# Two feed-forward chunks woven together, their seven products' shared sums kept in the accumulation banks

## The chip, the cores and the metric

The kernel runs on one core of a Trainium2 chip. The time is the device time of one execution in microseconds (us). The core's engines that matter here are TensorE (PE, the matrix products), VectorE (DVE), ScalarE (ACT), the SyncE queue that issues most transfers (SP) and GpSimd (POOL, which issues the accumulating transfers). Products accumulate in banks of PSUM; everything else lies in SBUF.

## The reference

An encoder trunk of two layers over 512 tokens of width 1024. Each layer mixes tokens in three ways (differential attention, a convolution module, a neighbourhood attention), adds the result to x, then a SwiGLU feed-forward block, then a gated per-layer input. The change touches the feed-forward block, its preparation in the output projection and two flags in the differential attention.

```python
D_MODEL, SEQ, DEPTH = 1024, 512, 2
D_FF = int(math.ceil(8 * D_MODEL / 3 / 256) * 256)          # 2816: 22 chunks of 128
...
        x = x + merged @ w_o[i]
        h = rmsnorm(x, norm_ffn[i])
        x = x + (jax.nn.silu(h @ w_ffn_gate[i]) * (h @ w_ffn_up[i])) @ w_ffn_down[i]
```

All operands are float32.

## The kernel before

Activations lie with the width on the 128 partitions: x and h are eight tiles of 128x512 (tokens along the free side). Every float32 operand of a product is split in a high and a low part (`split`: a copy on ScalarE, a subtraction on VectorE), and a product is three matmuls: high times high, high times low, low times high.

The feed-forward block works on 22 chunks of 128 hidden channels a layer, in three parts of 8, 7 and 7 (`PARTS`). After each part eight down blocks multiply the part's hidden channels with `w_ffn_down` (`gemm`, 128x512 matmuls; the first two as one `pair`), are scaled by the norm (`self.rb`) and added to x.

For one chunk, gate and up (two rows of blocks) times h (two halves of the width by two halves of the tokens) is a 2x2 block product, and `seven` makes it with seven products in place of eight. The weights' sums s1 to s4 and the tokens' sums t1 to t4 (`quarters`, in the output projection) are the operands beside the plain blocks. A product is 4 pairs x 3 = 12 matmuls of 128x256, so a chunk is 84. In the text a product is named by its two operands: "s3 t2" is s3 times t2.

The weights of a chunk come by transfer: s1 and s2 begin as plain loads on SyncE's queue and are completed by accumulating loads on GpSimd's (L987); g (a11, a12) and a22 are plain loads. `halve` splits them: a11/a12 and s1/s2 in rotating buffers `wh` and `wl` (three each, 128x1024), a22 in `kh` and `a`, s3/s4 in two fixed pairs, `pt` for even chunks and `y` for odd ones. s3 and s4 are VectorE sums in a `qk` tile. This preparation has a higher priority by 400 steps (`w_ahead`) than the rest.

The order on TensorE is the order in which the program is written; on the other engines and the transfer queues a scheduler orders the instructions by priority and due time. An engine carries its instructions out in that order.

Before, a chunk's products run without a break in the order a11 b11, a22 t4, s2 t1, a12 b21, s1 t3, s3 t2, s4 b22 (a layer's head chunk in another order). ScalarE copies three of them from their banks to SBUF (p1, p4, p5), and VectorE makes the gate and up sums with seven 128x256 operations (nine in the head chunk). `rest` (Silu, product of gate and up, split) is put off to the next chunk's third product. Chunks take their three banks in turn from the tags `mm, mm, mm` and `sc, sc, av`; `tr` is the tag of the transposition banks, which also serve the norm.

Of the kernel before, what the change touches and what calls it, by code (L numbers as in the profile page):

```python
# [12 lines left out]
F32R = mybir.dt.float32r  # L13
I32 = mybir.dt.int32
AF = mybir.ActivationFunctionType
# [5 lines left out]
P = 128  # L21
# [40 lines left out]
class Net:  # L62
# [109 lines left out]
            self.low = self.split(hi[:, :n], lo[:, :n], raw[:, :n])  # L172
        return hi, lo

    def mm3(self, out, wh, wl, ah, al, first, last):
        mm = self.nc.tensor.matmul
        mm(out, wh, ah, start=first, stop=False)  # L177
        mm(out, wh, al, start=False, stop=False)  # L178
        mm(out, wl, ah, start=False, stop=last)  # L179

    def gemm(self, out, ap, acts, first=True, last=True):

# [88 lines left out]
    def halves(self, h):  # L271
        return h if isinstance(h, tuple) else (h[:, 0, :], h[:, 1, :])

    def norm_chunk(self, k, x, g, tag, st):

        if k == KD - 1:
            self.sumsq(k, x, st)
        h = self.operand(x, g, tag)
        if k < KD - 1:
            self.sumsq(k, x, st)  # L280
        return h
# [562 lines left out]
    def diff_unit(self, head, qt, st4, k2, st, box, ys):  # L844

        nc, i = self.nc, self.i
        half, t = qt // 2, qt % 2
        box[qt] = self.probs(st4, k2, qt, box["s0"])
        if t == 0:
            return  # L850
        yield 3
        ats = [box[2 * half], box[2 * half + 1]]
        pps = []
        for kp in range(2):
            pt = self.ps("tr", (P, 2, 256))
# [12 lines left out]
        cs = slice((head % 2) * P, (head % 2) * P + P)  # L868
        for kp in range(2):
            for u in range(2):  # L870
                v = st["v", head // 2][kp][:, u].rearrange("p (a b) -> p a b", a=2)
                self.mm3(av[:, half * 256:half * 256 + 256], v[:, 0, cs], v[:, 1, cs],
                         pps[kp][:, 0, u], pps[kp][:, 1, u], kp * 2 + u == 0, kp * 2 + u == 3)
# [39 lines left out]
    def w_o(self, mg, xsrc):  # L913
        self.phase = "wo"
        xs, h, st, self.four = [], [], [], []
        self.zs = [self.parts_of("z", [2, 256], 2, F32R) for _ in range(4)]
        for m in range(KD):
            if m % 2 == 0:
                two = self.parts_of("x", [512], 2)
            xo = two[m % 2]  # L920
            self.nc.sync.dma_start(xo, xsrc[m])
            if m == 0:
                both = [self.ps("mm") for _ in range(2)]
                self.pair(both, self.a["w_o"][self.i, 0:2], mg)
# [12 lines left out]
        self.four.append(self.quarters(xs, h, 3))  # L937
        self.main_norm(st[0])
        return xs, h

    def quarters(self, x, h, j):
# [16 lines left out]
        self.tt(t4, t2, b21, ALU.subtract)  # L958
# [10 lines left out]
        return dict(b11=cut(ha, one), b21=cut(hb, one), b22=cut(hb, two),  # L969
                    **{f"t{n + 1}": (o[:, 0], o[:, 1]) for n, o in enumerate(d)})  # L970

    def seven(self, wg, wu, bs, tags, spare, md, first, fb):


        nc = self.nc
        with self.tc.high_priority(offset=min(self.w_ahead, self.tc.cur_priority - self.p0)):
# [34 lines left out]
        def product(out, w, b, first):  # L1011
            wh, wl = ws[w]
            mm = nc.tensor.matmul
            for k in range(4):
                c = slice(k * P, k * P + P)
                bh, bl = bs[k][b]
                mm(out, wh[:, c], bh, start=first and k == 0, stop=False, skip_group_check=True)  # L1017
                mm(out, wh[:, c], bl, start=False, stop=False, skip_group_check=True)  # L1018
                mm(out, wl[:, c], bh, start=False, stop=k == 3, skip_group_check=True)  # L1019
            self.chunk2()  # L1020

        o = self.sb("t", [P, 2, 256])
        p1, p4 = o[:, 0], o[:, 1]
        p5 = self.sb("a", [P, 256])
        gg, uu = self.sb("t", [P, 2, 256]), self.sb("t", [P, 2, 256])
        head = fb == 0
# [12 lines left out]
        product(Q[:, 0], "s1", "t3", False)  # L1039
        product(A[:, 1], "s3", "t2", True)  # L1040
        if head:
            self.tt(gg[:, 0], Q[:, 1], p1, ALU.add)
            self.tt(gg[:, 1], C[:, 0], p5, ALU.add)
        else:
            product(C[:, 0], "s4", "b22", False)
        rb = self.rb.rearrange("p (a b) -> p a b", a=2)
        self.tt(p5, p4, p5, ALU.subtract)
        self.tt(gg[:, 0], gg[:, 0] if head else A[:, 0], rb[:, 0], ALU.mult)
        self.tt(p1, A[:, 1], p1, ALU.subtract)
        self.tt(uu[:, 0], p1, Q[:, 0], ALU.subtract)  # L1050
        self.tt(uu[:, 1], uu[:, 0], p5, ALU.add)
        self.tt(gg[:, 1], gg[:, 1] if head else C[:, 0], p1, ALU.subtract)
        self.tt(gg[:, 1], gg[:, 1], rb[:, 1], ALU.mult)

        def rest(then):
            i = self.act(gg, gg, AF.Silu, table="silu")
# [3 lines left out]
            self.held = self.split(*self.halves(md), gg.rearrange("p a b -> p (a b)"))  # L1060

        self.pending.append(rest)

    def behind(self, i, then):

# [17 lines left out]
    def ffn(self, h, x):  # L1083
# [6 lines left out]
        md8.append(tuple(self.sb("e", [P, 512], F32R) for _ in range(2)))  # L1090
        self.sums, self.sevens = [t for _ in range(2) for t in self.parts_of("qk", [1024], 2)], 0
        for part in PARTS:
            mids = []
            for f, fb in enumerate(part):
                tags = (("mm", "mm", "mm"), ("sc", "sc", "av"))[fb % 2]
                md = md8[f]
                mids.append(md)
                wg, wu = self.a["w_fg"][i, fb], self.a["w_fu"][i, fb]
                self.seven(wg, wu, bs, tags, spare[fb % 2], md, part[0] and f < 2, fb)
            self.flush()  # L1100
            down = [self.a["w_fd"][i, m][:, part[0] * P:(part[-1] + 1) * P] for m in range(KD)]
            two = [self.ps(("mm", "sc")[fb % 2 == 0]) for _ in range(2)]
# [364 lines left out]
```

## Time and profile before

| | |
|---|---|
| median of 3 runs | 1776.36 us |
| range of the runs | 1776.2 to 1777.24 us |
| span of the profiled execution | 1776.7 us |
| TensorE clock granted | 0.999 |
| busy PE, DVE, ACT, POOL | 1767.5, 1421.7, 894.4, 103.0 us |
| feed-forward products, layer 1 | from 495.93 us; down blocks of part 0 from 577.09 us |

No time of the profiled execution but its span is shown; the span lies within the range of the runs. In rows of a timeline the columns are: start, duration, engine, line, operation, what is written and read, and in brackets the idle time before and what ended it. Rows of groups give the busy time, the mean of one in ns, and the idle time before with what ended it. Rows of waits give who waited on whom, the sum in us, how often, and the longest.

### The profile page before, as it was taken

Reading aid. Unit: us, or ns where it says so; the run is one execution under the profiler, and the core shown is the slowest. Engines: PE = TensorE matmul, PEld = TensorE weight load, DVE = VectorE, ACT = ScalarE, POOL = GpSimd, SP = SyncE. Lnnn points to the kernel's source line nnn. Section 1 sums busy time; section 2 is a strip of 40 time slices with the busy share of each in tenths; the row PEclk is TensorE's granted clock in tenths of the full one; section 3 lists DMA queues with packets and bytes.
Section 4 is the critical chain, followed back from the end, with each engine's and each line's share of the span. In section 5 each row is a group of like instructions: output and inputs, shape, how many; then the busy total and the mean of one; then the engine's idle time right before and its main releaser. Section 6 shows DMA issues by size and latency. Waiting matters only on the chain.

```text
span 1776.7 us, 27451 instructions
## 1 busy us (share of the span) xinstructions
PE 1767.5 (99%) x10210; PEld 1559.6 (88%) x10210; DVE 1421.7 (80%) x2418; ACT 894.4 (50%) x1561; POOL 103.0 (6%) x146
## 2 busy tenths in 40 slices
PE   9999999999999999999999999999999999999998
PEld 7888888888899899998888888888888998989987
DVE  7878887998798587787776788889887976867776
ACT  5577555225565254454545765452356643534454
POOL 0000000000111010100000000000001110101000
PEclk9999999999999999999999999999999999999999
DMA  5666641334757366543447655423357664655332
GB/s 202 188 186 176 161 125 42 113 98 140 230 150 193 109 167 160 132 131 123 145 124 198 176 165 149 113 71 95 93 179 198 171 179 115 173 144 151 98 108 92
DMA packets 113509, 256.07 MB, mean 144 GB/s; under 512 B 14560, under 2 KB 19424, under 8 KB 113376
## 3 DMA queue, kind: packets, MB, share of 16 engines
q1 hardware_dynamic: 99984, 229.93, 42.3%
q0 software_dynamic: 12672, 23.07, 8.3%
q8 instruction: 81, 1.33, 0.3%
q10 hardware_dynamic: 720, 1.31, 0.2%
q14 instruction: 52, 0.43, 0.1%
HBM read 215.46 MB, written 7.34 MB: 125 GB/s over the span
## 4 chain that ended last, share of the span: by engine, by line
PE 96%; DVE 2%; ACT 1%; issue 0%; DMA 0%; POOL 0%; ACTq 0%; POOLq 0%; DVEq 0%
PE ffn_mm L1017 4%; PE ffn_mm L1019 4%; PE ffn_mm L177 4%; PE ffn_mm L179 4%; PE ffn_mm L178 4%; PE ffn_mm L1018 4%; PE ffn_sc L1019 3%; PE ffn_sc L1017 3%; PE ffn_sc L1018 3%; PE mergea_mm L177 2%; PE mergea_mm L178 2%; PE mergea_mm L179 2%; PE diff_sc L811 2%; PE gatec_mm L177 2%; PE gatec_mm L178 2%; PE gatec_mm L179 2%
## 5 line engine op out<-in xcount | busy, mean ns | idle before, releaser
L160 DVE SCALAR_TENSOR_TENSOR conv_z<-glu_z,pre_par,conv_z 128x512 f32<-128x512 f32 x240 | 179.4, 748 | 3.3
L143 ACT ACTIVATE ffn_wh<-ffn_wr 128x1024 fp32r<-128x1024 f32 (+1 forms) x92 | 92.7, 1014 | 111.7 <-PE ffn_mm L178 77.1
L987 POOL DMA_DIRECT2D ffn_qk<-w_fu x88 | 78.0, 990 | 605.7 <-DMA ffn_qk<-w_fu 414.7
L157 DVE TENSOR_TENSOR ffn_wl<-ffn_wr,ffn_wh 128x1024 fp32r<-128x1024 f32 (+1 forms) x92 | 107.4, 1173 | 5.4 <-ACT ffn_wh L143 4.9
L157 DVE TENSOR_TENSOR ffn_t<-ffn_mm,wo_rb 128x512 f32<-128x512 f32 (+1 forms) x64 | 38.6, 604 | 67.9 <-PE ffn_mm L179 67.8
L143 ACT ACTIVATE mergea_wh<-mergea_wr 128x1024 fp32r<-128x1024 f32 (+1 forms) x32 | 27.1, 846 | 96.8 <-PE mergea_mm L178 79.6
L143 ACT ACTIVATE ffn_wh<-ffn_qk 128x1024 fp32r<-128x1024 f32 x44 | 46.7, 1060 | 35.9 <-PE ffn_mm L178 15.7
L157 DVE TENSOR_TENSOR ffn_wl<-ffn_qk,ffn_wh 128x1024 fp32r<-128x1024 f32 x44 | 53.8, 1224 | 11.3 <-ACT ffn_wh L143 11.3
L157 DVE TENSOR_TENSOR ffn_t<-ffn_t,ffn_t 128x512 f32<-128x512 f32 (+1 forms) x46 | 31.3, 680 | 31.4 <-ACT ffn_t L143 30.9
L143 ACT ACTIVATE diff_a<-diff_sc,diff_s 128x512 f32<-128x512 f32 x32 | 22.0, 686 | 61.0 <-DVE diff_s L902 61.0
L177 PE MATMUL ffn_mm<-ffn_v,ffn_wh 128*128 128x512 f32 x132 | 51.4, 389 | 0.0
L178 PE MATMUL ffn_mm<-ffn_v,ffn_wh 128*128 128x512 f32 x132 | 51.4, 389 | 0.0
L179 PE MATMUL ffn_mm<-ffn_v,ffn_wl 128*128 128x512 f32 x132 | 51.3, 389 | 0.0
L177 PE MATMUL ffn_mm<-ffn_y,ffn_wh 128*128 128x512 f32 x132 | 51.3, 389 | 0.0
L178 PE MATMUL ffn_mm<-ffn_y,ffn_wh 128*128 128x512 f32 x132 | 51.3, 389 | 0.0
L179 PE MATMUL ffn_mm<-ffn_y,ffn_wl 128*128 128x512 f32 x132 | 51.3, 389 | 0.0
L1019 PE MATMUL ffn_mm<-wo_h,ffn_wl 128*128 128x256 f32 x176 | 49.8, 283 | 0.0
L1019 PE MATMUL ffn_sc<-wo_h,ffn_wl 128*128 128x256 f32 x176 | 49.8, 283 | 0.0
L1018 PE MATMUL ffn_mm<-wo_h,ffn_wh 128*128 128x256 f32 x176 | 49.8, 283 | 0.0
L1018 PE MATMUL ffn_sc<-wo_h,ffn_wh 128*128 128x256 f32 x176 | 49.8, 283 | 0.0
L1017 PE MATMUL ffn_sc<-wo_h,ffn_wh 128*128 128x256 f32 x176 | 49.8, 283 | 0.0
L1017 PE MATMUL ffn_mm<-wo_h,ffn_wh 128*128 128x256 f32 x176 | 49.8, 283 | 0.0
(876 smaller groups left out, 6588.6 us busy)
## 6 DMA issues: line engine op xcount, KB each, us to landing
ffn_qk<-w_fu POOLq DMA_DIRECT2D x88, 256.0 KB, 5.7
ffn_wr<-w_fg SPq DMA_DIRECT2D x44, 512.0 KB, 3.7
ffn_wr<-w_fd SPq DMA_DIRECT2D x32, 448.0 KB, 3.9
ffn_r<-w_fu SPq DMA_DIRECT2D x44, 256.0 KB, 3.7
ffn_qk<-w_fg SPq DMA_DIRECT2D x44, 256.0 KB, 4.3
ffn_qk<-w_fu SPq DMA_DIRECT2D x44, 256.0 KB, 4.6
natten_wr<-w_in SPq DMA_DIRECT2D x16, 512.0 KB, 4.3
natten_b<-bias SPq DMA_DIRECT2D x32, 256.0 KB, 4.0
```

The costliest lines, as they stand in the source:

```text
L143: i = self.nc.scalar.activation(out, in_, func, **kw)
L157: return self.nc.vector.tensor_tensor(out, a, b, op)
L160: return self.nc.vector.scalar_tensor_tensor(out, a, s, b, op0, op1)
L177: mm(out, wh, ah, start=first, stop=False)
L178: mm(out, wh, al, start=False, stop=False)
L179: mm(out, wl, ah, start=False, stop=last)
L811: self.nc.tensor.matmul(out, st4[:, u, qs], st[:, ks], start=n == 0, stop=n == 1)
L987: nc.gpsimd.dma_start(q, wu[:, lo], accum_op=ALU.add)
L1017: mm(out, wh[:, c], bh, start=first and k == 0, stop=False, skip_group_check=True)
L1018: mm(out, wh[:, c], bl, start=False, stop=False, skip_group_check=True)
L1019: mm(out, wl[:, c], bh, start=False, stop=k == 3, skip_group_check=True)
```

## The change

In `seven`, products that share a term now share a bank. a11 b11 goes to bank C; ScalarE copies C to A, and a12 b21 is added on top of C (gate's left half). s3 t2 is added in A on top of the copy; ScalarE copies A to Q; s2 t1 is added in A, ScalarE copies it to SBUF; a22 t4 is added in Q, and s4 b22 in A. s1 t3 has a bank of its own, T, of the tag `tr`, from where ScalarE copies it to SBUF. VectorE is left with four 128x256 operations (five in a layer's head chunk, which keeps s4 b22 in another `tr` bank Z).

`seven` has become a generator with five stretches, and `sevens_of` runs two neighbouring chunks in turn: for chunk n and n+1 TensorE's order is a11 b11 of n+1; s2 t1, a22 t4 of n; s1 t3 of n+1; s4 b22 of n; s3 t2, a12 b21 of n+1. A part's first chunk runs its first three stretches alone, its last chunk its last two. A layer's head chunk runs a11 b11, s4 b22, a12 b21, s1 t3, s3 t2 before chunk 1 begins.

The sums t2 and t4 get the other sign, which the last addition to x undoes. In the output projection the operands of the even width tiles are made for the first 256 tokens only. In the differential attention the start flag is set once per bank.

```diff
-    def seven(self, wg, wu, bs, tags, spare, md, first, fb):
+    def seven(self, wg, wu, bs, tags, spare, md, first, fb, early):
...
-        A, C, Q = (self.ps(t, (P, 2, 256)) for t in tags)
+        C, A, Q = (self.ps(t, (P, 256)) for t in tags)
...
-        product(A[:, 0], "a11", "b11", True)
-        self.act(p1, A[:, 0], AF.Copy)
-        if head:
-            product(Q[:, 1], "a12", "b21", True)
-            product(C[:, 0], "s4", "b22", True)
-        product(Q[:, 0], "a22", "t4", True)
-        self.act(p4, Q[:, 0], AF.Copy)
-        five = C[:, int(head)]
-        product(five, "s2", "t1", True)
-        self.flush(self.act(p5, five, AF.Copy))
-        if not head:
-            product(A[:, 0], "a12", "b21", False)
-        product(Q[:, 0], "s1", "t3", False)
-        product(A[:, 1], "s3", "t2", True)
...
-        self.tt(p5, p4, p5, ALU.subtract)
-        self.tt(gg[:, 0], gg[:, 0] if head else A[:, 0], rb[:, 0], ALU.mult)
-        self.tt(p1, A[:, 1], p1, ALU.subtract)
-        self.tt(uu[:, 0], p1, Q[:, 0], ALU.subtract)
-        self.tt(uu[:, 1], uu[:, 0], p5, ALU.add)
-        self.tt(gg[:, 1], gg[:, 1] if head else C[:, 0], p1, ALU.subtract)
-        self.tt(gg[:, 1], gg[:, 1], rb[:, 1], ALU.mult)
+        def corner():
+            product(C, "a12", "b21")
+            if not early:
+                self.tt(gg[:, 0], C, self.halved(0), ALU.mult)
+
+        product(C, "a11", "b11", True)
+        self.act(A, C, AF.Copy)
+        yield
+        if early:
+            Z = self.ps("tr", (P, 256))
+            product(Z, "s4", "b22", True)
+            self.act(gg[:, 1], Z, AF.Copy)
+            corner()
+            yield
+        T = self.ps("tr", (P, 256))
+        product(T, "s1", "t3", True)
+        self.act(uu[:, 0], T, AF.Copy)
+        yield
+        product(A, "s3", "t2")
+        self.flush(self.act(Q, A, AF.Copy))
+        if not early:
+            corner()
+        yield
+        product(A, "s2", "t1")
+        self.act(uu[:, 1], A, AF.Copy)
+        product(Q, "a22", "t4")
+        self.tt(uu[:, 1], uu[:, 1], uu[:, 0], ALU.add)
+        self.tt(uu[:, 0], Q, uu[:, 0], ALU.add)
+        if early:
+            self.tt(gg[:, 0], C, self.halved(0), ALU.mult)
+            self.tt(gg[:, 1], A, gg[:, 1], ALU.add)
+        yield
+        if not early:
+            product(A, "s4", "b22")
+        self.tt(gg[:, 1], gg[:, 1] if early else A, self.halved(1), ALU.mult)
...
+    def sevens_of(self, pairs, head):
+        def go(*gens):
+            for g in gens:
+                next(g, None)
+
+        pairs = iter(pairs)
+        one = next(pairs)
+        go(one, one, one)
+        if head:
+            go(one)
+        for two in pairs:
+            go(two, one, two, one, two)
+            one = two
+        go(one, one)
...
-            h.append(self.norm_chunk(m, xo, self.par(self.i, "ffn", m), "h", st))
+            h.append(self.norm_chunk(m, xo, self.par(self.i, "ffn", m), "h", st, 512 if m % 2 else 256))
...
-        self.tt(t2, b22, t1, ALU.add)
+        self.stt(t2, t1, -1.0, b22, ALU.mult, ALU.subtract)
...
-                self.tt(x[m], x[m], d, ALU.add)
+                self.tt(x[m], x[m], d, ALU.subtract)
```

More of the change, by code (lines that the diff above doesn't have):

```diff
@@ L173, in weights, with mm3 @@
         return hi, lo
-    def mm3(self, out, wh, wl, ah, al, first, last):
+    def mm3(self, out, wh, wl, ah, al, first, last, **kw):
         mm = self.nc.tensor.matmul
-        mm(out, wh, ah, start=first, stop=False)
-        mm(out, wh, al, start=False, stop=False)
-        mm(out, wl, ah, start=False, stop=last)
+        mm(out, wh, ah, start=first, stop=False, **kw)
+        mm(out, wh, al, start=False, stop=False, **kw)
+        mm(out, wl, ah, start=False, stop=last, **kw)
     def gemm(self, out, ap, acts, first=True, last=True):
@@ L272, in halves, with norm_chunk @@
         return h if isinstance(h, tuple) else (h[:, 0, :], h[:, 1, :])
-    def norm_chunk(self, k, x, g, tag, st):
+    def norm_chunk(self, k, x, g, tag, st, n=512):
         if k == KD - 1:
             self.sumsq(k, x, st)
-        h = self.operand(x, g, tag)
+        if n < 512:
+            tag = tuple(a[:, :n] for a in self.halves(self.sb(tag, [P, 2, 512], F32R)))
+        h = self.operand(x[:, :n], g, tag)
         if k < KD - 1:
@@ L872, in diff_unit @@
                 self.mm3(av[:, half * 256:half * 256 + 256], v[:, 0, cs], v[:, 1, cs],
-                         pps[kp][:, 0, u], pps[kp][:, 1, u], kp * 2 + u == 0, kp * 2 + u == 3)
+                         pps[kp][:, 0, u], pps[kp][:, 1, u], half + kp + u == 0,
+                         half * kp * u == 1, skip_group_check=True)
         if half == 0:
@@ L955, in quarters @@
         self.tt(t1, b11, b12, ALU.subtract)
-        self.tt(t2, b22, t1, ALU.add)
+        self.stt(t2, t1, -1.0, b22, ALU.mult, ALU.subtract)
         self.tt(t3, b22, b12, ALU.subtract)
-        self.tt(t4, t2, b21, ALU.subtract)
+        self.stt(t4, t2, -1.0, b21, ALU.mult, ALU.subtract)
         if j < 2:
@@ L1008, in seven, with product @@
             halve(*spare, sums[1], ("s3", "s4"))
-        A, C, Q = (self.ps(t, (P, 2, 256)) for t in tags)
-        def product(out, w, b, first):
+        C, A, Q = (self.ps(t, (P, 256)) for t in tags)
+        def product(out, w, b, first=False):
             wh, wl = ws[w]
@@ L1034, in seven @@
-        five = C[:, int(head)]
-        product(five, "s2", "t1", True)
-        self.flush(self.act(p5, five, AF.Copy))
-        if not head:
-            product(A[:, 0], "a12", "b21", False)
-        product(Q[:, 0], "s1", "t3", False)
-        product(A[:, 1], "s3", "t2", True)
[L1041 to L1046, printed above, removed]
@@ L1062, in seven, with halved @@
         self.pending.append(rest)
+    def halved(self, n):
+        return self.rb[:, n * 256:n * 256 + 256]
+    def sevens_of(self, pairs, head):
[11 more added lines that the diff above has]
+        go(one, one)
     def behind(self, i, then):
@@ L1092, in ffn @@
         for part in PARTS:
[L1093 to L1099, printed above, removed]
+            mids = md8[:len(part)]
+            self.sevens_of((self.seven(self.a["w_fg"][i, fb], self.a["w_fu"][i, fb], bs,
+                                       (("mm", "mm", "mm"), ("sc", "sc", "av"))[fb % 2],
+                                       spare[fb % 2], md8[f], part[0] and f < 2, fb, fb == 0)
+                            for f, fb in enumerate(part)), part[0] == 0)
             self.flush()
             down = [self.a["w_fd"][i, m][:, part[0] * P:(part[-1] + 1) * P] for m in range(KD)]
-            two = [self.ps(("mm", "sc")[fb % 2 == 0]) for _ in range(2)]
+            two = [self.ps(("mm", "sc")[part[-1] % 2 == 0]) for _ in range(2)]
             self.pair(two, down[:2], mids)
```

4 lines of the change are left out of this document (removed).

## The prediction

> **What bounds the kernel now.** I read the page first (busy shares, then the chain that ended last), then TensorE's waits, then the windows of the feed-forward stage, and last its rows in time order.
>
> ```profile
> span 1776.7 us, 27451 instructions
> PE 1767.5 (99%) x10210; PEld 1559.6 (88%) x10210; DVE 1421.7 (80%) x2418; ACT 894.4 (50%) x1561; POOL 103.0 (6%) x146
> ...
> PE 96%; DVE 2%; ACT 1%; issue 0%; DMA 0%; POOL 0%; ACTq 0%; POOLq 0%; DVEq 0%
> ```
>
> TensorE is 99% busy and 96% of the chain. The page warns that a busy PE is not a PE at its peak, so the waits of PE are the better witness:
>
> ```profile
> PE pre_av L325 <- DVE pre_zeror L398: 1.1, 1, 1.1
> PE natten_tr L734 <- ACT natten_e L143: 0.3, 2, 0.2
> PE natten_tr L736 <- ACT natten_e L143: 0.3, 2, 0.2
> PE natten_tr L736 <- DVE natten_a L157: 0.2, 1, 0.2
> ```
>
> Those four rows are all of them: 1.9 us in the whole kernel, none in the feed-forward stage. All of that stage in layer 1:
>
> ```profile
> core 0: us, PE busy (x) PEld busy (x) DVE busy (x) ACT busy (x) POOL busy (x), PEclk, DMA share, GB/s
> 495.70:838.00 342.30, 342.30 (x2389) 321.55 (x2388) 266.19 (x424) 160.81 (x245) 33.00 (x37) 1.00 0.55 147
> ```
>
> PE is busy for every one of the 342.3 us, VectorE for 266, ScalarE for 161, the clock granted in full. The change keeps seven products of twelve matmuls, so PE's work here is the same count of the same shapes. A gain could only come out of gaps, and there are none: the stage can get slower or stay. What can make it slower is a product that reaches PE before its operand or its bank is ready.
>
> **VectorE and ScalarE: what is taken off and put on.** Each chunk loses three 128x256 operations on VectorE (seven to four), each layer's head chunk four (nine to five): 42x3 + 2x4 = 134. ScalarE gets one copy more per chunk and two more in the head chunks: 46.
>
> ```profile
> L157 DVE TENSOR_TENSOR ffn_t<-ffn_t,wo_rb 128x256 f32<-128x256 f32 x23 | 9.6, 418 | 0.0
> ...
> L143 ACT ACTIVATE ffn_wh<-ffn_wr 128x1024 fp32r<-128x1024 f32 x28 | 29.3, 1051 | 35.1 <-PE ffn_mm L178 29.6 <-issue 4.1 <-PE ffn_mm L1018 0.9
> ...
> L143 ACT ACTIVATE ffn_wh<-ffn_wr 128x896 fp32r<-128x896 f32 x16 | 15.0, 947 | 20.8 <-PE ffn_mm L178 11.0 <-PE ffn_sc L178 5.2 <-issue 3.6
> ...
> L143 ACT ACTIVATE ffn_t<-ffn_mm 128x256 f32<-128x256 f32 x22 | 8.1, 375 | 21.0 <-PE ffn_mm L1019 21.0
> ```
>
> That is 134 x 0.418 = 56 us less on VectorE and 46 x 0.375 = 17 us more on ScalarE, both beside PE. I cost both at nothing: no PE wait ends on VectorE here, and ScalarE is idle for half of the stage. The half-token operands of the even chunks (four per layer, ScalarE 128x512 to 128x256, VectorE likewise) lie in the output projection under PE and are also nothing; the sign flips only swap an operation for one of the same shape.
>
> **The copies in a steady cycle.** New on ScalarE is that the copies now stand between two products of PE: A<-C must be done before s3 t2, Q<-A before s2 t1 overwrites A, the copy of s2 t1's sum before s4 b22 overwrites A. ScalarE works in order, and the last of these stands behind the conversion of the weights two chunks on, which itself waits for s2 t1 to release its buffer. The nearest rows are the end of part 0, where before has the same wait for a release at the same product index:
>
> ```profile
> 574.41 1.04 ACT L143 ACTIVATE ffn_wh<-ffn_wr 128x1024 fp32r<-128x1024 f32 x1
> ...
> 574.22 0.28 PE L1017 MATMUL ffn_sc<-wo_rp,ffn_y 128*128 128x256 f32 x1
> ...
> 575.65 0.28 PE L1017 MATMUL ffn_sc<-wo_h,ffn_y 128*128 128x256 f32 x1
> ```
>
> Two products of PE start 1.43 us apart (574.22, 575.65): that is the unit. If s2 t1 ends at 574.22, the conversion runs from 574.41; activations overlap by some 0.09 (513.01 + 0.63 against 513.55 in the ramp's rows below), so the next starts at 575.36, and the copy takes 0.38 and ends at 575.74. In a steady cycle two products (a22 t4 and the next chunk's s1 t3) lie between, so s4 b22 wants the bank at 574.22 + 2.87 = 577.09: 1.35 us to spare. A<-C has three to four products in hand, Q<-A two. Cost nothing; the cover is those 1.35 us.
>
> **The end of a part.** There only a22 t4 lies between, and s4 b22 wants the bank at 575.65, 0.09 before the copy is done; with the 896-wide weights of parts 1 and 2 the conversion is 0.1 shorter (947 against 1051 ns above) and it just fits. I take 0.1 to 0.15 for part 0 and 0.05 for the others: 0.25 a layer, 0.5 in all, with ends 0 and 0.55 for each of six (a conversion half as late again), 0 to 3.3. At the start of a part one product lies between a11 b11 and s3 t2: the copy is done 0.2 + 0.38 = 0.58 after the first, wanted after 1.43, no wait. The weights of a part's first two chunks are made under the down blocks, where ScalarE mostly waits. The head chunk also puts two products into the transposition banks; the second, s1 t3, waits for the norm's reduction to leave its bank:
>
> ```profile
> 499.60 0.68 DVE L216 TENSOR_REDUCE wo_sm<-wo_tr 128x4 f32<-128x512 f32 x1
> ```
>
> It ends at 500.28, and s1 t3, the fourth product, starts 13 products before the 17th, which starts at 519.72 (next rows): 519.72 - 13 x 1.435 = 501.06, less one set of four small transpositions that lies between. Nothing, with ends of 0 and 0.7 (the reduction's own length) a layer.
>
> **The ramp: the term that decides.** Interleaving asks for weights sooner. Counted in products from the start of a layer's stage, s3 t2 of the third chunk was the 20th (two chunks of seven, then its sixth); now it is the 17th (five of chunk 0, then 0 and 1 and then 1 and 2 interleaved). The 17th product starts at 519.72, the 20th at 524.02:
>
> ```profile
> 519.72 0.28 PE L1017 MATMUL ffn_mm<-wo_rp,ffn_wh 128*128 128x256 f32 x1
> 519.84 0.28 PE L1018 MATMUL ffn_mm<-wo_rp,ffn_wh 128*128 128x256 f32 x1
> 519.95 0.28 PE L1019 MATMUL ffn_mm<-wo_rp,ffn_wl 128*128 128x256 f32 x1
> ...
> 524.25 0.28 PE L1019 MATMUL ffn_mm<-wo_rp,ffn_pt 128*128 128x256 f32 x1
> ```
>
> Its third matmul needs the low half of the s3/s4 weights. In before that half is made late, behind the first Silu and its table load:
>
> ```profile
> 511.31 0.38 ACT L143 ACTIVATE ffn_a<-ffn_sc 128x256 f32<-128x256 f32 x1 [0.65 <-PE ffn_sc L1019]
> 511.71 1.28 ACT L143 ACT_TABLE_LOAD   x1
> 513.01 0.63 ACT L143 ACTIVATE ffn_t<-ffn_t 128x512 f32<-128x512 f32 x1
> 513.55 1.04 ACT L143 ACTIVATE ffn_wh<-ffn_qk 128x1024 fp32r<-128x1024 f32 x1
> ...
> 519.15 1.06 ACT L143 ACTIVATE ffn_pt<-ffn_qk 128x1024 fp32r<-128x1024 f32 x1 [3.10 <-DVE ffn_qk L157]
> ...
> 513.67 0.69 DVE L157 TENSOR_TENSOR ffn_t<-ffn_t,ffn_t 128x512 f32<-128x512 f32 x1 [1.52 <-ACT ffn_t L143]
> 514.62 1.22 DVE L157 TENSOR_TENSOR ffn_wl<-ffn_qk,ffn_wh 128x1024 fp32r<-128x1024 f32 x1 [0.26 <-ACT ffn_wh L143]
> 515.76 1.22 DVE L157 TENSOR_TENSOR ffn_wl<-ffn_wr,ffn_wh 128x1024 fp32r<-128x1024 f32 x1
> 516.90 0.68 DVE L157 TENSOR_TENSOR ffn_v<-ffn_t,ffn_v 128x512 fp32r<-128x512 f32 x1
> 517.50 0.68 DVE L157 TENSOR_TENSOR ffn_qk<-ffn_qk,ffn_r 128x512 f32<-128x512 f32 x1
> ...
> 520.25 1.23 DVE L157 TENSOR_TENSOR ffn_pt<-ffn_qk,ffn_pt 128x1024 fp32r<-128x1024 f32 x1
> ```
>
> In before it is ready at 521.48 and wanted at 524.25, 2.77 to spare; three products earlier are 4.30. The table load follows the copy of the tenth product (511.31) in both programs, so this chain starts at the same time. The rows give the steps: 1.14 from one 128x1024 operation to the next on VectorE (514.62 to 515.76), 0.60 for a 128x512 one (516.90 to 517.50). The changed order on VectorE, as its listing has it, is then: low half of s1/s2 (514.62), the finished activations' low half (515.76), the sum s3 (516.36), the low half of the fourth chunk's a11/a12 (516.96), the sum s4 (518.10 to 518.78). The a11/a12 are there in time: their conversion waits for s2 t1 of chunk 1, the 13th product, which ends three products before the 17th starts, 515.42; 0.19 and 1.05 later it is 516.66. ScalarE converts s3/s4 at 518.81 to 519.87; VectorE, after one 128x512 and two 128x256 operations (0.60 and twice 0.34), makes the low half from 519.98 to 521.21. Wanted at 519.95: PE stands for about 1.3 us. A standing PE holds all products behind it, so the whole 1.3 goes into the time. The transfers keep their order on SyncE's and GpSimd's queues, and the conversion at 513.55 followed the Silu without a wait for a landing, so raw weights are not what is late. Of the other products of the ramp, the tightest is the same chunk's s1 t3 (low half ready 515.84; the 15th product's third matmul 517.09); from the fourth chunk on there are over 1.5 us, helped by the stall itself. Layer 2 has the same chain at the same distances (ready at 1399.80 + 1.23, wanted at 1403.81, 2.78 to spare):
>
> ```profile
> 1399.80 1.23 DVE L157 TENSOR_TENSOR ffn_pt<-ffn_qk,ffn_pt 128x1024 fp32r<-128x1024 f32 x1
> ...
> 1403.81 0.28 PE L1019 MATMUL ffn_mm<-wo_rp,ffn_pt 128*128 128x256 f32 x1
> ```
>
> So 2 x 1.3 = 2.6 us. Bounds: nothing, if the freed VectorE brings the chain 1.3 earlier (the Silu at 513.01 leaves room for that); 2 x 2.4 if another long operation, 1.14, gets ahead of the sum s4.
>
> **A rule of the skill.** ScalarE's copies from bank to bank have no row here; the nearest is 0.375 from a bank to SBUF, which I take. The Trainium skill, ScalarE: Activation LUTs, "Step-by-step: what each stage is for", holds that an activation ends sooner into PSUM than into SBUF. By that rule the 0.5 us at the part ends would go, for 1779.0 in place of 1779.4; no row of before can show it.
>
> **Sum.** 2.6 + 0.5 = 3.1 us on the span of 1776.7. The span is the profiled execution's time as far as shown and lies 0.3 over the median of the runs, 1776.36; on the median I give 1779.4. One measurement can tell about 0.2%, 3.55 us, from no change, so the forecast lies just inside (1779.9).
>
> **Rivals.**
> (a) The ramp is covered: the sum s4 or the conversion comes a microsecond earlier than my walk, and nothing is left but the part ends: 1776.9. For it: VectorE has 0.42 us less per removed operation. Against: the chain starts at the table load, and its VectorE order is long operations.
> (b) Slower: the part ends cost their upper bound, because the third down weight's raw data or an activation in front is late and the copy stands behind it: 6 x 0.55 + 2.6 = 5.9, 1782.3. For it: nothing to spare there. Against: in before that conversion starts 0.19 after its release.
> (c) Slower: ScalarE's order holds the copy in each cycle. It decides from the point where the conversion ahead starts more than 1.35 us late (raw weights late, or a wait for VectorE's low half). At 0.2 us in each of 38 steady cycles (19 pairs of neighbouring chunks a layer), 7.6 + 3.1: 1787.1. The Trainium skill, TensorE: Matmul & The Clock Gate, "Architectural detail", says that ScalarE's and VectorE's queues are strictly first in, first out, so nothing passes such a conversion; the trace agrees, its copies never start ahead of a waiting conversion. Against it: the stage's ScalarE is idle for half the time.
> (d) Faster: VectorE's 56 us were on the path somewhere. Against: the waits of PE are 1.9 us in all and lie outside, so this gives 1774.5 at best; under 1772.8 (0.2%) PE's own pace would have to change, which is the other half of this case. That the change does not do what it says belongs here too: if the counts did not fall, nothing would be gained, and nothing is counted as gained.
>
> **How the numbers follow.** Forecast (1777.5 to 1781.5) 0.48, of which 0.34 under the bound of 0.2% (1779.9); (a) 0.17; (b) 0.14; (c) 0.16; (d) 0.05. Slower: 0.14 + 0.14 + 0.16 = 0.44. Same: 0.34 + 0.17 = 0.51. Faster: 0.05. The range reaches from just under (a) to (c), 1775.9 to 1787, and leaves out (d) and the upper half of (c) and little else.
>
> **What would show it.** In the profile after: VectorE's count 134 down, ScalarE's 46 up; in PE's waits one row of about 1.3 us in each layer on VectorE's low half into the s3/s4 tile, at the 17th product; small rows on ScalarE's copy at the six part ends; none in steady cycles. Wrong would be: PE waits on ScalarE's copies in many cycles (then c), no wait at the 17th product (then a), or a longer wait there with a conversion or a landing ahead of the sum s4.

## The result, and the profile after

The changed kernel takes 1781.16 us (median of 10 runs, 1779.79 to 1783.06), the kernel before beside it on the same chip 1776.54 (10 runs): a ratio of 1.0027, 95% interval 1.0018 to 1.0036. That is 4.6 us slower, within the forecast's own range (1777.5 to 1781.5), and a little past the 0.2% that tell from no change, where the forecast of 1779.4 lay a little short of it.

The page after, its first lines:

```profile
span 1778.5 us, 27425 instructions
PE 1768.7 (99%) x10210; PEld 1559.0 (88%) x10210; DVE 1376.2 (77%) x2284; ACT 915.0 (51%) x1607; POOL 108.8 (6%) x146
```

VectorE has 134 operations less, ScalarE 46 more, as counted. VectorE is busy for 45.5 us less, and the kernel became slower. The span is only 1.8 over that of before, less than the runs say; the last experiment shows why spans mislead here. Of PE's waits one is new (the row has who waited on whom, the sum in us, how often, the longest):

```profile
PE ffn_mm L1022 <- DVE ffn_pt L157: 2.0, 2, 1.0
```

The 1.1 us of PE on `pre_zeror` and the short waits of the neighbourhood attention were there before. The view of windows of layer 1, before and then after (length, then PE's busy time), runs from the first feed-forward product to the same matmul of the per-layer input in both kernels, some 12 us behind the last down block; this is what "the stage" means below:

```profile
495.93:849.37 353.44, 353.44 (x2442) 330.79 (x2441) 271.65 (x435) 164.61 (x251) 34.03 (x38) 1.00 0.54 145
```
```profile
495.19:850.69 355.50, 354.45 (x2442) 331.04 (x2441) 249.80 (x368) 175.93 (x274) 36.96 (x39) 1.00 0.53 144
```

The stage grew by 2.06 us; in layer 2 by 2.08 (353.44 to 355.52). Together 4.1 of the 4.6 us; the rest is inside the interval (3.2 to 6.4 us). PE's busy column falls short of the length by 1.05 only, half of it: a matmul is on record for 0.28 us while the next starts 0.12 after it, so the first tenths of a stop don't count as idle. The distance from one start to the next shows it all. Rows of the ramp in layer 1, first VectorE and ScalarE, then PE:

```profile
516.33 1.22 DVE L157 TENSOR_TENSOR ffn_wl<-ffn_wr,ffn_wh 128x1024 fp32r<-128x1024 f32 x1
517.47 0.68 DVE L157 TENSOR_TENSOR ffn_qk<-ffn_qk,ffn_wr 128x512 f32<-128x512 f32 x1
518.07 0.68 DVE L157 TENSOR_TENSOR ffn_a<-ffn_r,ffn_kh 128x512 fp32r<-128x512 f32 x1
518.18 1.06 ACT L143 ACTIVATE ffn_pt<-ffn_qk 128x1024 fp32r<-128x1024 f32 x1
518.67 0.42 DVE L157 TENSOR_TENSOR ffn_t<-ffn_t 128x256 f32<-128x256 f32 x1
519.19 0.42 DVE L157 TENSOR_TENSOR ffn_t<-ffn_av,ffn_t 128x256 f32<-128x256 f32 x1
519.53 1.22 DVE L157 TENSOR_TENSOR ffn_pt<-ffn_qk,ffn_pt 128x1024 fp32r<-128x1024 f32 x1
```
```profile
518.85 0.28 PE L1021 MATMUL ffn_sc<-wo_h,ffn_y 128*128 128x256 f32 x1
518.97 0.28 PE L1022 MATMUL ffn_sc<-wo_h,ffn_y 128*128 128x256 f32 x1
519.30 0.38 PE L1020 MATMUL ffn_mm<-wo_rp,ffn_pt 128*128 128x256 f32 x1
519.52 0.28 PE L1021 MATMUL ffn_mm<-wo_rp,ffn_pt 128*128 128x256 f32 x1
520.80 0.39 PE L1022 MATMUL ffn_mm<-wo_rp,ffn_pt 128*128 128x256 f32 x1 [1.00 <-DVE ffn_pt L157]
521.03 0.28 PE L1020 MATMUL ffn_mm<-wo_rp,ffn_pt 128*128 128x256 f32 x1
```

VectorE does what the prediction's walk listed, in that order: low half of the fourth chunk's weights, sum s4, and after shorter ones the low half of s3/s4. PE's starts are 0.12 apart in a run (518.85, 518.97). The 17th product's first matmul comes 0.33 after its forerunner (ScalarE's high half ends at 519.24), the second 0.22, the third 1.28 (VectorE's low half ends at 520.75), the next 0.23. Over the pace that is 0.21 + 0.10 + 1.16 + 0.11 = 1.58 us. The waits row shows 1.0 of them, counted from the end of the matmul before.

The end of part 0 has the other piece, no row of the waits but a late start:

```profile
575.36 1.05 ACT L143 ACTIVATE ffn_wh<-ffn_wr 128x1024 fp32r<-128x1024 f32 x1
576.31 0.36 ACT L143 ACTIVATE ffn_t<-ffn_sc 128x256 f32<-128x256 f32 x1
```
```profile
576.49 0.28 PE L1022 MATMUL ffn_av<-wo_z,ffn_a 128*128 128x256 f32 x1
576.72 0.38 PE L1020 MATMUL ffn_sc<-wo_h,ffn_y 128*128 128x256 f32 x1
576.95 0.28 PE L1021 MATMUL ffn_sc<-wo_h,ffn_y 128*128 128x256 f32 x1
```

The conversion of the third down weight stands ahead of the copy; the copy ends at 576.67, and s4 b22 starts 0.23 after the matmul before it, its second matmul another 0.23: 0.11 twice, 0.22. At the ends of parts 1 and 2 one start comes 0.20 after the last, 0.08 each. That is 0.38 a layer. 1.58 + 0.38 is 1.96 of the 2.06. The last 0.1 lies in the head chunk, at the norm's second set of four small transpositions:

```profile
500.23 4.01 POOL L223 TENSOR_TENSOR wo_rc<-wo_sm,pre_power 128x4 f32<-128x4 f32 x1 [4.95 <-DVE wo_sm L219]
```
```profile
504.30 0.65 PE L227 MATMUL wo_tr<-pre_ident,wo_rc 128*128 128x128 f32 x4
```

They read what GpSimd's power makes, which ends at 504.24; the first starts 0.19 after the matmul before it (504.11) and the second 0.16 later, where before has 0.12 and 0.11. In before the same power lasts 1.14 us and is done over three microseconds ahead; the changed kernel's takes 4.01, in both layers. That is 0.12 a layer, and with it the gaps add up to the stage's growth within 0.02 us. Why the power takes so long here is open. No steady cycle has a late start.

### The profile page after: what moved, and what is told of

Read it like the earlier page. It is cut to its first block, busy times and chain, and to the rows that moved or that the text cites. A ratio compares the mean times of both kernels' runs of the same rounds, so it can differ in the third digit from the quotient of the medians.

```text
span 1778.5 us, 27425 instructions
## 1 busy us (share of the span) xinstructions
PE 1768.7 (99%) x10210; PEld 1559.0 (88%) x10210; DVE 1376.2 (77%) x2284; ACT 915.0 (51%) x1607; POOL 108.8 (6%) x146
## 4 chain that ended last, share of the span: by engine, by line
PE 95%; DVE 2%; ACT 1%; issue 1%; DMA 0%; POOL 0%; ACTq 0%; POOLq 0%; DVEq 0%
PE ffn_mm L177 4%; PE ffn_mm L178 4%; PE ffn_mm L179 4%; PE ffn_mm L1022 3%; PE ffn_mm L1020 3%; PE ffn_mm L1021 3%; PE ffn_sc L1020 3%; PE ffn_sc L1022 3%; PE ffn_sc L1021 3%; PE mergea_mm L179 2%; PE mergea_mm L177 2%; PE mergea_mm L178 2%; PE diff_sc L813 2%; PE gatec_mm L177 2%; PE gatec_mm L178 2%; PE gatec_mm L179 2%
## 5 line engine op out<-in xcount | busy, mean ns | idle before, releaser
L157 DVE TENSOR_TENSOR ffn_t<-ffn_mm,wo_rb 128x512 f32<-128x512 f32 (+1 forms) x86 | 47.8, 556 | 71.0 <-PE ffn_mm L179 60.7
L143 ACT ACTIVATE natten_wh<-natten_wr 128x1024 fp32r<-128x1024 f32 x24 | 25.4, 1058 | 41.4 <-issue 15.2
```

What stands on the lines that cost most here:

```text
L143: i = self.nc.scalar.activation(out, in_, func, **kw)
L157: return self.nc.vector.tensor_tensor(out, a, b, op)
```

## The experiments

Theory: the 1.6 and the 0.4 are the whole cost. The ramp's part is the order on VectorE behind the table load; the ends' part is the copy behind the conversion; in the steady cycles 1.35 us hide the copies. (The 0.1 at the head was not part of the theory.) Rivals: the copies cost something in each cycle; or the half-token operands, the head's bank or PE's pace have a share that no wait shows.

**1. The low half of s3/s4 before the fourth chunk's.** One long operation is taken out of the way in the ramp:

```diff
-            halve(*spare, sums[1], ("s3", "s4"))
+            self.low34 = halve(*spare, sums[1], ("s3", "s4"))
...
+            if fb == 3:
+                self.behind(i, self.low34)
```

> The changed kernel with one order more: the low half of chunk 3's a11/a12 is put behind the low half of chunk 2's s3/s4 on VectorE; nothing else. Theory (the ramp stall is VectorE's order before the 17th product): the s4 sum and the low half come about 1.05 us earlier, PE's stop at the 17th product falls from 1.58 us a layer (gaps over the pace, the wait itself 1.17) to about 0.5, the time from 1781.2 to about 1779.0. Rival (the time sits in ScalarE's copies of every cycle): the stop may shrink in the trace, the time stays at 1781 within 0.5. Rival (raw weights land late): the stop stays, with a landing as its cause.

1778.77 us, ratio 1.0013 (1.0004 to 1.0022); the stage 354.44 and 354.46, so 1.06 a layer less than in the changed kernel. The wait and its releaser stay, shorter:

```profile
PE ffn_mm L1024 <- DVE ffn_pt L157: 0.5, 2, 0.3
```
```profile
518.52 1.23 DVE L157 TENSOR_TENSOR ffn_pt<-ffn_qk,ffn_pt 128x1024 fp32r<-128x1024 f32 x1 [0.19 <-ACT ffn_pt L143]
519.66 1.22 DVE L157 TENSOR_TENSOR ffn_wl<-ffn_wr,ffn_wh 128x1024 fp32r<-128x1024 f32 x1
```

VectorE now waits for ScalarE's high half: the chain behind the table load is what remains.

**2. The table load out of that chain.** A Silu of 128x4 elements in the head chunk makes the table load come there:

```diff
         self.flush(self.act(Q, A, AF.Copy))
+        if fb == 0:
+            self.act(self.sb("sm", [P, 4]), self.ident[:, :4], AF.Silu, table="silu")
```

> The changed kernel with a four-element Silu in the head chunk of each layer, so that the table load (1.28 us) is done before the first Silu needs it. Theory (the chain to the 17th product begins at the table load): the chain is 0.8 to 1.3 us earlier, no wait for the s3/s4 low half is left or under 0.1, the stage loses about 1.5 us a layer, time about 1778.0. Rival (copies in every cycle): 1781 within 0.5, whatever the stop does.

1777.22 us, ratio 1.0004 (0.9995 to 1.0012); the stage 353.82 and 353.81. No wait of the feed-forward is left in PE's waits. The load lies eleven microseconds earlier, and the low half is there 0.47 before the 17th product's third matmul (519.20):

```profile
500.16 1.28 ACT L143 ACT_TABLE_LOAD   x1
```
```profile
515.43 0.69 DVE L157 TENSOR_TENSOR ffn_qk<-ffn_qk,ffn_wr 128x512 f32<-128x512 f32 x1
516.04 1.22 DVE L157 TENSOR_TENSOR ffn_wl<-ffn_wr,ffn_wh 128x1024 fp32r<-128x1024 f32 x1
...
517.51 1.22 DVE L157 TENSOR_TENSOR ffn_pt<-ffn_qk,ffn_pt 128x1024 fp32r<-128x1024 f32 x1
```

The ramp's wait is gone whole, but this edit moved two things. The chain runs 1.02 us earlier (the finished activations' low half starts at 514.11 in place of 515.13, with the stage's start all but the same), and the scheduler now puts the sum s4 ahead of the fourth chunk's low half, as it stood in experiment 1 too; of the 2.02 us that the low half comes earlier, each gives about half. The earlier chain alone was not run; by these numbers, an estimate, it would have left some 0.6 us of the 1.58. Of the 1.68 us a layer that are gone, 1.58 are the ramp and 0.1 the head's transpositions: GpSimd's power lasts 2.87 here and ends before it is wanted. The 0.38 of the part ends stay.

**3. The part ends alone.** The conversion of the third down weight is put behind the copy:

```diff
-        self.act(uu[:, 1], A, AF.Copy)
+        self.last = self.act(uu[:, 1], A, AF.Copy)
...
+                    self.hold = self.last if m == 2 else None
```

In `weights`, the conversion is held behind `self.hold` where there is one.

> The changed kernel with the conversion of the third down weight put behind the copy of s2 t1 at the end of each part. Theory (part ends cost 0.22, 0.08 and 0.08 us a layer because the copy stands behind that conversion): those gaps go, the stop at the 17th product stays, time 1780.5 to 1780.8. Rival (b of the prediction, the ends are worth several us): 1778 or less.

1780.25 us, ratio 1.0019 (1.0011 to 1.0028); the stage 355.12 and 355.11, 0.37 and 0.41 less than in the changed kernel. The runs' intervals overlap with the changed kernel's, here and in experiments 6 and 9; the stage's length, which repeats to 0.01 us in the profiles of before and of experiments 10 and 11, decides. The copy now goes first, and the gaps at the part ends are gone:

```profile
576.45 0.39 ACT L143 ACTIVATE ffn_t<-ffn_sc 128x256 f32<-128x256 f32 x1
576.73 1.05 ACT L143 ACTIVATE ffn_wh<-ffn_wr 128x1024 fp32r<-128x1024 f32 x1
```

**4. The same copies without the interleaving.** Each chunk runs its five stretches before the next begins, so every chunk end is like a part's:

```diff
-        for two in pairs:
-            go(two, one, two, one, two)
-            one = two
-        go(one, one)
+        go(one, one)
+        for two in pairs:
+            go(two, two, two, two, two)
```

> The changed kernel without the interleaving: every chunk's products run alone in the order a11 b11, s1 t3, s3 t2, a12 b21, s2 t1, a22 t4, s4 b22; banks, copies and sums as changed. Theory (the interleaving is the cover for ScalarE's copies): each of the 38 chunks that is not the last of its part now has the wait that only the part's last had, 0.2 us each with a 1024-wide conversion ahead of the copy, about 0.9 for the two a layer where the a22 conversion stands ahead too; s3 t2 of chunk 2 is again the 17th product and its low half 0.7 us later: 8 + 3 + 1.5 over 1781.2, about 1793. Rival (the interleaving itself is what costs, by asking for weights sooner): under 1781.

1793.61 us, ratio 1.0098 (1.0084 to 1.0112); the stage 361.58 and 361.59. PE now waits on ScalarE's copies:

```profile
PE ffn_sc L1020 <- ACT ffn_t L143: 2.6, 2, 1.3
PE ffn_mm L1020 <- ACT ffn_t L143: 1.9, 2, 1.0
...
PE ffn_mm L1022 <- DVE ffn_pt L157: 0.9, 2, 0.4
```

An ordinary chunk end costs the 0.22 of the part end above; at two of them in a layer a22's conversion slips in front of the copy and they cost 1.56 and 1.23. The interleaving, which brings over half of the ramp's wait (2.0 us of PE's waits with it, 0.9 without), is what pays for the copies: without it the bill is four times as high.

**5. The first three edits together.**

> The changed kernel with three edits together: the low half of the s3/s4 weights of chunk 2 first on VectorE in the ramp, the first Silu's table load asked for one product earlier, and the third down weight's conversion behind the copy at the end of a part. Theory (a late low half in the ramp and a late copy at the part ends are the whole cost): the feed-forward stage is as long as before, 353.4 to 353.6 us in each layer against 355.50 and 355.52 in the changed kernel, and no wait of PE is left in it; 1776.5 to 1777.2 us. Rival (some of the difference lies elsewhere: in the half-token operands, in the head's transposition bank, in a slower pace with ScalarE writing to banks): 1777.8 or more, with the stage longer than before although no wait shows.

1776.53 us (11 runs) against 1776.35, ratio 1.0000 (0.9991 to 1.0009). The stage of layer 1, on the view of windows:

```profile
495.26:848.70 353.44, 353.44 (x2442) 330.76 (x2441) 249.98 (x368) 176.38 (x275) 35.76 (x39) 1.00 0.54 145
```

To the hundredth what it was before; layer 2 the same. So the ramp, the part ends and the head's transpositions, whose gap went with the table load, are the whole cost: what else the change does, taken together, costs nothing, be it by the operands, by a bank or by the pace. It ties with before and does not beat it, although VectorE is busy 250 us of the stage in place of 272: PE had no gap there that could close.

**6. Without the half-token operands.**

```diff
-            h.append(self.norm_chunk(m, xo, self.par(self.i, "ffn", m), "h", st, 512 if m % 2 else 256))
+            h.append(self.norm_chunk(m, xo, self.par(self.i, "ffn", m), "h", st))
```

> The changed kernel with full-token feed-forward operands for the even width tiles, as before the change. Theory (the half-token operands are worth nothing, the work lies under PE in the output projection): 1780.7 to 1781.7 us, the feed-forward stage 355.5 in each layer, and ScalarE and VectorE busy longer by some 4 x 2 times the difference between a 128x512 and a 128x256 operation. Rival (the half operands save time at the ramp): 1782 or more; (they cost time): 1780.3 or less.

A miss: 1782.20 us, ratio 1.0030 (1.0019 to 1.0040); the stage 356.00 and 356.03, 0.5 a layer longer than with them. The time goes at the head, in front of s1 t3 and of the norm's transpositions:

```profile
500.04 0.69 DVE L216 TENSOR_REDUCE wo_sm<-wo_tr 128x4 f32<-128x512 f32 x1
...
500.87 0.39 PE L1020 MATMUL ffn_tr<-wo_v,ffn_wh 128*128 128x256 f32 x1
```
```profile
505.17 0.28 PE L1022 MATMUL ffn_sc<-wo_h,ffn_wl 128*128 128x256 f32 x1
505.61 0.65 PE L227 MATMUL wo_tr<-pre_ident,wo_rc 128*128 128x128 f32 x4 [0.16 <-POOL wo_rc L223]
```

VectorE, with more to do for the operands, ends the norm's reduction at 500.73, and the product that takes its bank waits for it (0.14, and 0.10 for the matmul behind it, which is late too: the wake-up of PE); GpSimd's power for the norm follows later too, since VectorE's step in front of it now stands behind two 128x1024 operations (3.1 us later in the stage), so that PE's transpositions start 0.44 after the matmul before them in place of 0.19. In the changed kernel the reduction ends at 499.74 and the product starts at 499.93.

**7. Too many copies in a steady cycle.** To measure the cover, the copy of s2 t1's sum is repeated in 18 chunks a layer (not the head chunk, not the last of a part):

```diff
-        self.act(uu[:, 1], A, AF.Copy)
+        for _ in range(4 if fb not in (0, 7, 14, 21) else 1):
+            self.act(uu[:, 1], A, AF.Copy)
```

> The changed kernel with ScalarE's copy of s2 t1's sum carried out four times in place of once, in 18 steady chunks a layer (not the head chunk, not the last chunk of a part). Three extra copies of about 0.30 us, 0.9 us a cycle, under the 1.35 to 1.4 us that the copy has to spare before s4 b22 overwrites the bank. Theory: no wait in the steady cycles, 1780.7 to 1781.7 us as the changed kernel, ScalarE busy about 40 us longer. Rival (ScalarE's order already holds the cycle): at least 0.3 us in each of 36 cycles, 1792 or more.

A miss: 1791.36 us, ratio 1.0083 (1.0069 to 1.0097), close to what the rival had, but not by its mechanism, as experiments 8 and 9 show. A cycle's rows on ScalarE in the changed kernel, then with four copies, then PE's with four:

```profile
546.63 1.06 ACT L143 ACTIVATE ffn_wh<-ffn_wr 128x1024 fp32r<-128x1024 f32 x1 [1.00 <-DMA ffn_wr<-w_fd]
547.60 0.37 ACT L143 ACTIVATE ffn_t<-ffn_mm 128x256 f32<-128x256 f32 x1
```
```profile
547.53 1.06 ACT L143 ACTIVATE ffn_wh<-ffn_wr 128x1024 fp32r<-128x1024 f32 x1 [0.95 <-PE ffn_mm L1021]
548.50 0.78 ACT L143 ACTIVATE ffn_t<-ffn_mm 128x256 f32<-128x256 f32 x2
549.17 0.62 ACT L143 ACTIVATE ffn_kh<-ffn_r 128x512 fp32r<-128x512 f32 x1
549.70 0.79 ACT L143 ACTIVATE ffn_t<-ffn_mm 128x256 f32<-128x256 f32 x2
```
```profile
550.18 0.28 PE L1022 MATMUL ffn_tr<-wo_z,ffn_wl 128*128 128x256 f32 x1
550.54 0.39 PE L1020 MATMUL ffn_mm<-wo_h,ffn_pt 128*128 128x256 f32 x1
```

Copies into the same tile don't overlap (two take 0.78), and a22's conversion went in between. The last copy ends 2.96 after the conversion's start (547.53 to 550.49), in the changed kernel 1.34 (546.63 to 547.97): not 0.9 but 1.62 us more. PE stands 0.24 ahead of s4 b22 and 0.10 at its next matmul. So the cover is 1.62 - 0.24 = 1.38 us, where the prediction had 1.35.

**8. Seven copies.**

> As the run with four copies, but seven: 1.8 us of extra copies a cycle, over the 1.35 to 1.4 us to spare by 0.4 to 0.6 with the wake-up of PE. Theory: PE waits on ScalarE's copy ahead of s4 b22 in each of 36 steady cycles, 36 x 0.4 to 0.6 = 14 to 22 us over the changed kernel: 1795 to 1804 us. Rival (the cover is larger than the rows say, or the next cycle makes the time good): 1783 or less.

Again a miss in size: 1842.91 us, ratio 1.0372 (1.0358 to 1.0386), far more than expected, for the same reason, and in the same place, all 36 cycles:

```profile
PE ffn_sc L1020 <- ACT ffn_t L143: 28.1, 18, 2.5
PE ffn_mm L1020 <- ACT ffn_t L143: 25.5, 18, 1.5
```

The next chunk's copy of s1 t3 went between them as well, the last copy ended 4.34 us after the conversion's start, 3.0 later than in the changed kernel, and PE stood 1.62 + 0.10 us in 28 of the 36 cycles: 3.0 less 1.38. The stage grew by 31 and 30 us.

**9. Three copies**, the amount just under the cover.

> As the run with four copies, but three. In the run with four the extra copies took 0.39 us each and not 0.30, and the 0.60 us conversion of a22 came in between them: the last copy ended 1.62 us later after the start of the weights' conversion than in the changed kernel, and PE stood 0.24 us ahead of s4 b22 (and 0.10 at its next matmul), so the cover is 1.38 us. With three copies the last one should end 1.62 - 0.39 = 1.23 us later. Theory (a cover of 1.35 to 1.4 us a cycle): no wait ahead of s4 b22 in any steady cycle, 1780.7 to 1781.7 us as the changed kernel. Rival (each microsecond put on ScalarE there costs in proportion, no threshold): three quarters of the four copies' 10.2 us less the extra conversion, 1786 or more.

1780.76 us, ratio 1.0022 (1.0013 to 1.0031); the stage 355.34 and 355.35. With 1.2 us more on ScalarE in each of 36 cycles there is no wait in any: the last copy is done at 549.06, 2.54 after the conversion's start, and s4 b22 starts on time at 549.28:

```profile
548.68 0.38 ACT L143 ACTIVATE ffn_t<-ffn_mm 128x256 f32<-128x256 f32 x1
```
```profile
549.16 0.28 PE L1022 MATMUL ffn_tr<-wo_z,ffn_wl 128*128 128x256 f32 x1
549.28 0.28 PE L1020 MATMUL ffn_mm<-wo_h,ffn_pt 128*128 128x256 f32 x1
```

Nothing, 0.24, 1.62 us for 1.2, 1.6, 3.0 us more: a threshold, not a price for each microsecond.

**10. Only the half-token operands, on the kernel before.**

> The kernel before with only the half-token operands of the even width tiles put in. Theory (they save time only where the head chunk's products use the transposition bank that the norm uses, as the run without them showed: 0.5 us a layer; before has no such wait): no change, 1776.0 to 1776.9 us, the feed-forward stage 353.4 in each layer. Rival (they are worth 0.5 us a layer by themselves): 1775.4 or less, with the stage at or under 353.0.

1777.11 us against 1776.74, ratio 1.0002 (0.9993 to 1.0011); the stage 353.44 in both layers. They are worth nothing there, 0.5 us a layer where the head's products use the norm's bank.

**11. The kernel before again.**

> The kernel before once more, for its profile alone: the feed-forward stage should again be 353.4 us in each layer to some hundredths, while the first products' stretch (26.4 us in the first profile) and the tail after the last product (7.08 us) may differ by up to a microsecond if they belong to the execution and not to the kernel. Rival (they belong to the kernel): 26.4 and 7.1 again.

The span is 1774.0 in place of 1776.7, and the stage what it was:

```profile
495.11:848.56 353.45, 353.45 (x2442) 330.77 (x2441) 271.82 (x435) 164.70 (x251) 34.00 (x38) 1.00 0.54 144
```

It starts at 495.11 in place of 495.93, and the tail after PE's last matmul is 5.47 us in place of 7.08. In all other profiles of this case that tail is 5.45 to 5.53. So 7.08 belonged to one execution, and the span of before, on which the prediction's sum stood, was some 2 us long by chance. The stages' lengths, not the spans, agree with the runs: over before, both layers together and the run's median,

| run | stages | median of the runs |
|---|---|---|
| after | +4.1 | +4.6 |
| low half first | +2.0 | +2.0 |
| table load early | +0.7 | +0.5 |
| part ends | +3.4 | +3.5 |
| no interleaving | +16.3 | +16.9 |
| three edits | 0.0 | +0.2 |
| no half tokens | +5.2 | +5.9 |
| four, seven, three copies | +14.7, +65.0, +3.8 | +15.0, +66.6, +4.0 |
| half tokens alone | 0.0 | +0.4 |

## Why the prediction was right, and where it was off

**The mechanism** was the one walked: the third chunk's s3 t2 as the 17th product, PE standing on VectorE's low half at its third matmul, once in each layer. Experiment 1 shortens that wait by VectorE's order alone, experiment 2 ends it by the earlier chain and that order together: both were named in the walk. Rivals (a), covered, and (d), faster, fall with the row itself; (b) with experiment 3, which finds 0.4 a layer at the part ends and not 1.65.

**The ramp was mis-sized**, 1.58 in place of 1.3 a layer. 0.10 is the wake-up of PE after a stop, which the sum did not have. The rest is VectorE: the addition of 519.19, which writes what the one ahead of it reads, began 0.10 after that one's end (518.67 and 0.42) where neighbours else start 0.08 before it, so the low half came 0.18 later. The product whose bank it reads, the 14th, had ended some three microseconds earlier, so the operation ahead is left as the cause. The prediction took 0.34 from start to start for both additions. It also had the high half ready at 519.87 for a matmul at 519.72 and passed over it; PE stood 0.21 there, without a cost of its own, since the low half came later still.

**The part ends**, 0.25 a layer, measured 0.38: part 0 0.22 against 0.1 to 0.15, half of it again the wake-up; the others 0.08 against 0.05. Ramps and ends together: 3.1 forecast, 3.9 from these gaps; with the head's 0.2, which the sum had at nothing, 4.1, as the stages' lengths have it.

**The steady cycles**, nothing, held with their price: 1.35 us of cover worked out, 1.38 measured, and rival (c) would begin at the point that the prediction gave; the experiments reached it with repeated copies and not, as (c) had it, with a late conversion. The half of (c) that rests on order is true: the Trainium skill, TensorE: Matmul & The Clock Gate, "Architectural detail", has ScalarE strictly first in, first out. The traces agree: at the end of part 0 the last matmul of s2 t1 was over at 575.35, and its copy still waited until 576.31 behind the conversion.

**The half-token operands and the head's bank** were each put at nothing, and the two are one term. The prediction gave the head's bank 0 to 0.7 without naming its cover; experiment 6 finds 0.5 a layer more without the half-token operands, and experiment 10 that they are worth nothing by themselves: they are that cover. It is not a full one, as the 0.12 a layer at the transpositions stays, and PE waits there for GpSimd's power, which the prediction did not look at, and not for a bank.

**VectorE's relief** came out at 45.5 us and not 56, mainly since neighbouring operations start 0.34 apart while each lasts 0.418. 1.4 of the 45.5 are the half-token operands (1377.6 us busy without them, 1376.2 with them), which leaves 0.33 for each of the 134. ScalarE's extra work is 20.6 us where 17 were forecast. Neither had a bearing on the time.

**The rule of the Trainium skill** (ScalarE: Activation LUTs, "Step-by-step: what each stage is for") was put at the wrong copy: the one late at the part ends goes from a bank to SBUF, so nothing there could shrink by it. Rows for both kinds now exist, bank to bank and bank to SBUF:

```profile
L143 ACT ACTIVATE ffn_mm<-ffn_mm 128x256 f32<-128x256 f32 x44 | 16.2, 368 | 20.0 <-PE ffn_mm L1022 18.8 <-DVE wo_x L157 1.2
...
L143 ACT ACTIVATE ffn_t<-ffn_mm 128x256 f32<-128x256 f32 x22 | 8.1, 367 | 0.0
```

368 and 367 ns: at this size the trace shows no gain from a bank as the destination.

**The sign.** Most of the forecast's own chance, 0.34 of 0.48, was put under the bound of 0.2%, with a sum 0.5 us short of it and terms whose bounds went mostly up. What the sum lacked, 0.6 us at the ramps, 0.3 at the part ends and 0.2 at the head, took it over, with 0.5 of the runs' difference that no stage shows.

## What to carry to other kernels

Where the matrix engine has no gaps, an edit that unloads another engine gains nothing there and can move deadlines: look for the operand that is asked for sooner, count from the start of the stage in products, and walk the order of the engine that makes it, with the wait of each step on the way. When an edit changes what a scheduler sees, read the new order before crediting the edit's own purpose. Price a stop as the lateness plus the wake-up, and judge a cover by repeating the covered work until it shows. Compare the lengths of stages between profiles, not their spans.

## What the runs showed of the hardware

- After a stop of PE in the feed-forward products the next matmul of 128x256 starts 0.20 to 0.23 us after the one that waited in place of 0.12: some 0.1 us beside the wait itself. At the ends of parts 1 and 2 only a late second matmul (0.20) was seen; experiment 3 takes it away with the order of the copy, but what delays a second matmul with no late first is open. Before has such ones too, behind both sets of the norm's transpositions.
- A table load costs its 1.28 us on ScalarE and no more here: in the prediction's rows it runs from 511.71, and the Silu behind it starts at 513.01.
- ScalarE's activations into different tiles start up to 0.1 us before the last one ends; repeated ones into the same tile do not overlap (two 128x256 copies in 0.78 us).
- PE's waits and busy time are told from the recorded ends of matmuls, which lie past the next start: 2.0 us in the waits of the ramp were 3.2 from start to start.
- GpSimd's power of 128x4 took 1.14 us at the head of before, 4.01 in the changed kernel, 2.87 in experiments 2 and 5 and 1.46 in experiment 6, with other work on VectorE beside it each time. What held it is not shown. In the changed kernel PE's transpositions start 0.06 behind its end, which bears the long span out.
